# Gate/up weight lows by accumulating transfers, activations kept in DRAM, sums shared between two engines, in a hybrid decoder layer

## The chip, the cores and the metric

The kernel runs on one core of one Trainium2 chip. The metric is the device time of one execution in microseconds (us), and the number compared is the median over runs. A core has five engines that run their own instruction streams and wait for each other by semaphores: TensorE (PE in the profile; PEld is its weight load), VectorE (DVE), ScalarE (ACT), GpSimd (POOL) and SyncE (SP, which here only issues transfers). Transfers between DRAM and the on-chip memory are carried by 16 DMA engines.

## The reference

One decoder layer in float32 over 512 tokens of width 1024: a mixer (dilated attention and retention side by side), cross attention to a memory of 256 tokens, and a gated feed-forward block of hidden width 2816. Each block normalises its input, and normalises its output before it is added to the running `x`. The change lies mostly in the last block:

```
def swiglu(h, w_gate_up, w_down):
    g, u = jnp.split(h @ w_gate_up, 2, axis=-1)
    return (jax.nn.silu(g) * u) @ w_down
...
y = swiglu(rms_norm(x, pre_ffn_g[l]), w_gate_up[l], w_down[l])
x = x + rms_norm(y, post_ffn_g[l])
```

## The kernel before

**Precision.** TensorE multiplies operands of type fp32r, which keep fewer bits than float32. Each float32 operand is therefore held as a high part (`h` at the end of the tile's name: the value cast to fp32r) and a low part (`l`: the value minus its high part), and each product is three matmuls, high by high, high by low and low by high (`mm3`, L84 to L86). The helper `split` makes the two parts: ScalarE casts (L90), VectorE subtracts (L91).

**The feed-forward block.** The hidden width is cut into 22 pieces of 128. For each piece `f` one 1 MB block of weights holds four quarters `a11, a12, a22, a21` of 512 columns each. The first two pieces are computed plainly (`plain`, `plain_load`). The other 20 run in `step(f)`, which takes seven products of half the tokens instead of eight (a Strassen form). Some products use quarters of the weights as they are (`wa`), some use sums of quarters (`sums`, then split into `wb`: s1 = a21 + a22, s3 = a11 - a21, s2 = s1 - a11, s4 = a12 - s2); likewise for the activations (`B11`, `B21`, `B22`, `T1` to `T4`). Each product is 4 x 3 matmuls of 128x128 by 128x256. They accumulate in three PSUM banks, `p`, `q` and `r`, each holding two products side by side.

In `step(f)` TensorE runs products 1, 2, 4, 6, 5, 7, 3. The seventh product writes the first half of `p` again, so it must wait until ScalarE has copied that half (L879) and VectorE has read the other half of the same bank (L883). The third product writes the second half of `r`, behind VectorE's read of the first (L920). Between these, the same step prepares weights for later pieces: GpSimd makes the four sums of block `f + 2` (L116 to L119), ScalarE and VectorE split `wa` and `wb` of block `f + 1` (`blocks_split`, four calls), SP fetches block `f + 3` (L108). It also finishes the piece before: VectorE adds (L887), ScalarE applies Silu (L888), VectorE multiplies gate and up into the activation tile `af` (L894).

**What sets the order.** The steps run inside `tc.manual_schedule()` (L985): there each engine executes its instructions in the order in which the program writes them, so an instruction that waits holds up all that stands behind it on its engine. Everywhere else a planner orders the instructions by their place in the program and by what is ready. Tiles come from pools with a fixed number of buffers; a tile that takes a freed buffer waits for the last user of that buffer. `up` has 20 buffers of 8 KB a partition; `rawp` has two for each of its tags (`raw`, `sums`).

**Behind the steps** comes the down projection: 11 weight chunks (`w_dn`), each fetched, split and multiplied; activations are split by `split_a` (ScalarE casts L1002, GpSimd subtracts L1003). The last four chunks are done block of tokens by block of tokens, and behind each block `residual` (L645) takes squares on ScalarE, a reciprocal root on VectorE, and adds to `x`. Ahead of the feed-forward block, `mem_block` does the same for cross attention, and `to_b` transposes the normed tokens and makes the `B` and `T` operands.

Of the kernel before, what the change touches and what calls it, by code (L numbers as in the profile page):

```python
# [19 lines left out]
P = 128  # L20
# [18 lines left out]
def hybrid_layer(ctx, tc, t, out):  # L39
# [59 lines left out]
    loaded = {}  # L99
# [3 lines left out]
    blocks = {}  # L103

    def blocks_fetch(f):
        chunks.remove(("w_gu", f))
        raw = rawp.tile([P, 2048], F32, tag="raw", name=uname("raw"))
        nc.sync.dma_start(raw, t["w_gu"][f])  # L108
        blocks[f] = [raw]

    def blocks_sum(f):
        raw = blocks[f][0]
        a11, a12, a22, a21 = (raw[:, i * 512:(i + 1) * 512] for i in range(4))
        sums = rawp.tile([P, 2048], F32, tag="sums", name=uname("sums"))
        s2, s4, s1, s3 = (sums[:, i * 512:(i + 1) * 512] for i in range(4))
        nc.gpsimd.tensor_add(s1, a21, a22)  # L116
        nc.gpsimd.tensor_sub(s3, a11, a21)
        nc.gpsimd.tensor_sub(s2, s1, a11)
        nc.gpsimd.tensor_sub(s4, a12, s2)  # L119
        blocks[f] += [sums, pair("wa"), pair("wb")]  # L120

    def blocks_split(f, i):
        raw, sums, wa, wb = blocks[f]
        src, w, c0, n = ((raw, wa, 1024, 512), (raw, wa, 0, 1024), (sums, wb, 1024, 1024), (sums, wb, 0, 1024))[i]
        split(src[:, c0:c0 + n], *part(w, c0, n))

    def load(pieces=1, swap=False):
        key = chunks.pop(0)
        src = t[key[0]][key[1]]
        raw = rawp.tile([P, 2048], F32, tag="raw", name=uname("raw"))  # L130
        w = pair("w")
        n = 2048 // pieces
        for i in range(pieces):
            c = slice(i * n, (i + 1) * n)
            nc.sync.dma_start(raw[:, c], src[:, c])
# [509 lines left out]
    def residual(pss, b, g, e=None, cuts=((0, 512), (512, 512))):  # L645
# [4 lines left out]
        for i, (c0, n) in enumerate(cuts):  # L650
            c = slice(c0, c0 + n)
            ps = pss[c0 // 512][:, c0 % 512:c0 % 512 + n]
            nc.scalar.activation(junk()[:, :n], ps, AF.Square, accum_out=ss[:, i:i + 1])
            e.tensor_scalar(v, ss[:, i:i + 1], 1.0 / D, v if i else EPS, op0=ALU.mult, op1=ALU.add)
            nc.vector.tensor_mul(z[:, c], ps, g[:, c])
# [159 lines left out]
    def mem_block(b, mid=None):  # L815
        e = nc.vector
        residual(out_proj((b,), o_lhs, wo, nat, "o2", 0, mid)[b], b, g3, e)
        return normed(b, g4, e)

    def to_b(h, b):  # L820
# [15 lines left out]
        b12 = work("b12").rearrange("p (k s) -> p k s", k=4)  # L836
        split(pv[0], *bview("B12", c0))
        split(pv[1], *bview("B22", c0))
        nc.vector.tensor_sub(t1, pv[0], braw[:, 0, :, c0:c0 + P])
        nc.scalar.copy(b12, pv[0])  # L840
        nc.vector.tensor_sub(t2, pv[1], t1)
        nc.vector.tensor_sub(t3, pv[1], b12)
# [12 lines left out]
    af = []  # L855
# [14 lines left out]
    def ffn_p12(f):  # L870

        w, p = blocks[f][2:], bank("p")
# [16 lines left out]

    def ffn_mult(f):  # L890
        s1, c, u = ffn.pop(f)[2:5]
        if f % 4 == 0:
            af.append(unit("af"))
        nc.vector.tensor_mul(af[-1][:, (f % 4) * S:(f % 4 + 1) * S], c, u)  # L894

    def step(f):
        nxt = f + 1 < FT
        ffn_p12(f)
        w, p, s1, c, u = ffn[f]
        if f + 2 < FT:  # L900
            blocks_sum(f + 2)
        if f > PRE:
            ffn_done(f - 1)
        if nxt:
            blocks_split(f + 1, 0)
# [11 lines left out]
        product(6, w, r[:, :H])  # L917
        if nxt:
            blocks_split(f + 1, 2)
        nc.vector.tensor_add(s1[:, H:], s1[:, :H], r[:, :H])  # L920
        product(5, w, q[:, H:])
        if nxt:
            blocks_split(f + 1, 3)
# [6 lines left out]
        del blocks[f]  # L930
# [24 lines left out]
    for f in range(PRE):  # L955
        for j in range(2):
            plain(f, j, 0, pg[f][j])
        if f == 0:
            late_splits = [to_b(hb, 2)]
# [171 lines left out]
```

## Time and profile before

| | us |
|---|---|
| median of 3 runs | 834.13 (832.35 to 834.33) |
| the profiled execution, its own time | 835.61 |
| its span, first to last instruction | 833.8 |
| TensorE busy in the span | 797.6 |
| VectorE | 553.2 |
| ScalarE | 351.0 |
| GpSimd | 245.8 |

Rows of the profile read: line of the kernel, engine, operation, output tile `<-` input tiles, shapes, count, then busy time and mean time of one. In a row of the timeline the first number is the start in us from the span's start and the second the time it took; brackets give how long the engine was idle just before and what ended that. In a row of the waits: who waited `<-` for whom, total us, times, longest. In a row of windows: the stretch, then busy time and instruction count of each engine, the granted TensorE clock as a share of full speed, the mean busy share of the DMA engines, and GB/s. Consecutive matmuls overlap, so their pace is read from their starts, not from their durations.

### The profile page before, as it was taken

What the parts mean: (1) busy time and instruction counts of PE and PEld (TensorE: products, weight loads), DVE (VectorE), ACT (ScalarE), POOL (GpSimd) and SP (SyncE); (2) the same over time, 40 slices, a digit from 0 to 9 for tenths busy, and PEclk for the clock granted to TensorE, in tenths of its full rate; (3) what the DMA queues carried; (4) which work ended last, traced back from release to release, by engine and by line L of the source; (5) the groups of instructions that cost most, each with busy time, mean ns of one, the idle gap of its engine ahead of it and who ended that gap; (6) DMA issues with size and microseconds to landing.
All of it is one profiled execution on the core that took longest, in us unless ns stands there. A gap on an engine that the chain in (4) does not pass through costs nothing.

```text
span 833.8 us, 12068 instructions
## 1 busy us (share of the span) xinstructions
PE 797.6 (96%) x4828; PEld 698.0 (84%) x4828; DVE 553.2 (66%) x1012; ACT 351.0 (42%) x615; POOL 245.8 (29%) x190
## 2 busy tenths in 40 slices
PE   9979999999999999999999999989999899999996
PEld 7768888877777878999988989988889889888884
DVE  6595168764566657667568888889988886631244
ACT  6504333466464723446434734333344335524110
POOL 0261024410110100400029165555565542326000
PEclk9998999999999999999999999999999999999998
DMA  9516212221124440515004032222222224641011
GB/s 335 233 51 243 85 51 90 71 93 52 51 90 178 188 152 5 197 52 202 2 26 152 27 119 84 101 101 102 88 69 97 101 102 177 233 170 51 1 50 51
DMA packets 16648, 90.18 MB, mean 108 GB/s; under 512 B 2000, under 2 KB 2000, under 8 KB 8016
## 3 DMA queue, kind: packets, MB, share of 16 engines
q1 hardware_dynamic: 15872, 88.35, 28.9%
q10 hardware_dynamic: 720, 1.06, 0.3%
q8 instruction: 38, 0.62, 0.3%
q14 instruction: 18, 0.15, 0.1%
HBM read 85.21 MB, written 4.19 MB: 107 GB/s over the span
## 4 chain that ended last, share of the span: by engine, by line
PE 53%; DVE 29%; issue 8%; ACT 5%; POOL 3%; DMA 2%; DVEq 0%; SPq 0%; ACTq 0%; POOLq 0%
DVE wal L91 7%; PE dn L85 5%; PE dn L86 5%; PE dn L84 5%; DVE af L894 3%; DVE wl L91 3%; DVE wbl L91 3%; PE o L85 2%; PE o L86 2%; PE o L84 2%; PE oT L507 2%; DMA raw<-in_w_out 1%; PE q L85 1%; PE q L86 1%; PE q L84 1%
## 5 line engine op out<-in xcount | busy, mean ns | idle before, releaser
L91 DVE TENSOR_TENSOR wl<-raw,wh 128x1024 fp32r<-128x1024 f32 (+1 forms) x91 | 112.9, 1273 | 69.0 <-ACT wh L90 45.2
L90 ACT CAST wh<-raw 128x1024 fp32r<-128x1024 f32 (+1 forms) x91 | 90.3, 1039 | 73.0 <-DMA raw<-in_w_in 36.6
L91 DVE TENSOR_TENSOR wal<-raw,wah 128x512 fp32r<-128x512 f32 (+1 forms) x40 | 66.4, 1661 | 24.7 <-ACT wah L90 24.7
L85 PE MATMUL dn<-wl,ah 128*128 128x512 f32 x176 | 68.6, 390 | 0.3 <-DVE wl L91 0.3
L86 PE MATMUL dn<-wh,al 128*128 128x512 f32 x176 | 68.5, 389 | 0.0
L84 PE MATMUL dn<-wh,ah 128*128 128x512 f32 x176 | 67.7, 389 | 0.0
L888 ACT ACTIVATE c<-c 128x512 f32<-128x512 f32 x20 | 12.6, 632 | 124.6 <-DVE c L887 124.6
L91 DVE TENSOR_TENSOR wbl<-sums,wbh 128x1024 fp32r<-128x1024 f32 x40 | 57.0, 1425 | 0.0
L116 POOL TENSOR_TENSOR sums<-raw 128x512 f32<-128x512 f32 x20 | 25.9, 1294 | 91.6 <-DMA raw<-in_w_gu 66.6
L1003 POOL TENSOR_TENSOR al<-af,ah 128x512 fp32r<-128x512 f32 x22 | 32.8, 1519 | 54.6 <-ACT ah L1002 54.5
L84 PE MATMUL p<-bB,wah 128*128 128x256 f32 x160 | 45.3, 283 | 0.0
L85 PE MATMUL p<-bB,wah 128*128 128x256 f32 x160 | 45.3, 283 | 0.0
L86 PE MATMUL p<-bB,wal 128*128 128x256 f32 x160 | 45.3, 283 | 0.0
L90 ACT CAST wbh<-sums 128x1024 fp32r<-128x1024 f32 x40 | 39.9, 1049 | 0.0
L85 PEld LDWEIGHTS dn<-wl,ah 128*128 128x128 f32 x176 | 33.0, 188 | 7.7 <-DVE wl L91 0.7
L84 PEld LDWEIGHTS dn<-wh,ah 128*128 128x128 f32 x176 | 33.0, 188 | 6.8
L86 PEld LDWEIGHTS dn<-wh,al 128*128 128x128 f32 x176 | 33.0, 188 | 6.7
L84 PE MATMUL p<-bT,wbh 128*128 128x256 f32 x80 | 23.8, 298 | 14.3 <-DVE c L883 14.3
L119 POOL TENSOR_TENSOR sums<-raw,sums 128x512 f32<-128x512 f32 x20 | 36.2, 1810 | 1.6
L85 PE MATMUL q<-hhl,wh 128*128 128x256 f32 x128 | 36.2, 284 | 0.2 <-DVE hhl L91 0.2
L84 PE MATMUL q<-hhh,wh 128*128 128x256 f32 x128 | 35.8, 284 | 0.3 <-ACT hhh L90 0.3
L86 PE MATMUL q<-hhh,wl 128*128 128x256 f32 x128 | 36.1, 283 | 0.0
(330 smaller groups left out, 2569.8 us busy)
## 6 DMA issues: line engine op xcount, KB each, us to landing
raw<-in_w_gu SPq DMA_DIRECT2D x22, 1024.0 KB, 4.8
raw<-in_w_in SPq DMA_DIRECT2D x12, 1024.0 KB, 4.8
raw<-in_w_dn SPq DMA_DIRECT2D x11, 1024.0 KB, 4.7
raw<-in_w_kv SPq DMA_DIRECT2D x8, 1024.0 KB, 4.7
x<-in_x SPq DMA_DIRECT2D x4, 1024.0 KB, 8.8
raw<-in_w_out SPq DMA_DIRECT2D x4, 1024.0 KB, 5.6
raw<-in_w_q SPq DMA_DIRECT2D x4, 1024.0 KB, 4.8
raw<-in_w_o SPq DMA_DIRECT2D x4, 1024.0 KB, 4.8
```

Of the source, the lines that this page charges most:

```text
L84: nc.tensor.matmul(o, lhsT=sh, rhs=mh, start=start, stop=False)
L85: nc.tensor.matmul(o, lhsT=sh, rhs=ml, start=False, stop=False)
L86: nc.tensor.matmul(o, lhsT=sl, rhs=mh, start=False, stop=stop)
L90: nc.scalar.copy(hi, src)
L91: nc.vector.tensor_sub(lo, src, hi.bitcast(F32))
L116: nc.gpsimd.tensor_add(s1, a21, a22)
L119: nc.gpsimd.tensor_sub(s4, a12, s2)
L507: nc.tensor.matmul(oTb[pr][rows, kb * P:S], lhsT=av[:, kb * 512 + h * AD:kb * 512 + (h + 1) * AD], rhs=u[:, off[kb]:off[kb] + S - kb * P], ...
L888: nc.scalar.activation(c, c, AF.Silu)
L894: nc.vector.tensor_mul(af[-1][:, (f % 4) * S:(f % 4 + 1) * S], c, u)
L1003: nc.gpsimd.tensor_sub(lo[:, c], af[i][:, c], hi[:, c].bitcast(F32))
```

## The change

1. The low part of `wa` is no longer a subtraction on VectorE (or on GpSimd for the two plain pieces). ScalarE writes the high part and then its negative into the low tile, and a transfer issued by GpSimd adds the weights from DRAM onto it (`accum_op=ALU.add`). This is done for block `f + 2` in step `f`, so three pairs of `wa` are alive.
2. Of the four sums s1 and s2 move to VectorE; s3 and s4 stay on GpSimd. The `sums` tile comes from the pool `up`.
3. The product of gate and up is stored to a DRAM tile `ad` by SP and loaded back by `split_a` in the down stage.
4. The fetch of block `f + 3` is issued at the start of the step; in the last three steps it fetches the first chunks of `w_dn`, the first of which is split in the last step, and the first activations are split between the last two steps.
5. In `residual` the multiplication by the gain stands ahead of the operation that waits for the squares. `mem_block` runs its residual and norm at high priority. `to_b` of the third token block does its subtractions on GpSimd, with ScalarE copying out of PSUM.
6. The DRAM loads of `x` stand behind the loop over chunks, and the reserved DMA scratch goes back to its default size.

```
+    def blocks_sum(f, names):
+        if f not in sums:
+            sums[f] = unit("sums")
...
+            e = nc.gpsimd if name in ('s3', 's4') else nc.vector
...
+    def blocks_a(f, n=1536, m=768):
+        w = was[f] = pair("wa")
+        for c0 in range(0, n, m):
+            c = slice(c0, c0 + m)
+            nc.scalar.copy(w[0][:, c], raws[f][:, c])
+        for c0 in range(0, n, m):
+            c = slice(c0, c0 + m)
+            nc.scalar.mul(w[1][:, c], w[0][:, c].bitcast(F32), -1.0)
+        nc.gpsimd.dma_start(w[1][:, :n], t["w_gu"][f][:, :n], accum_op=ALU.add)
+
+    def blocks_b(f, i):
+        if f not in wbs:
+            wbs[f] = pair("wb")
+        split(sums[f][:, i * 1024:(i + 1) * 1024], *part(wbs[f], i * 1024, 1024))
...
+            nc.vector.tensor_mul(z[:, c], ps, g[:, c])
             e.tensor_scalar(v, ss[:, i:i + 1], 1.0 / D, v if i else EPS, op0=ALU.mult, op1=ALU.add)
-            nc.vector.tensor_mul(z[:, c], ps, g[:, c])
...
+        pss = out_proj((b,), o_lhs, wo, nat, "o2", 0, mid)[b]
+        with tc.high_priority(600):
+            residual(pss, b, g3, nc.vector)
+            return normed(b, g4, nc.vector)
...
+    def keep(f, v):
+        nc.sync.dma_start(ad[:, f * S:(f + 1) * S], v)
+
     def ffn_mult(f):
...
+        c, u = ffn.pop(f)[3:5]
+        nc.vector.tensor_mul(c, c, u)
+        keep(f, c)
 
     def step(f):
         nxt = f + 1 < FT
+        two = f + 2 < FT
         ffn_p12(f)
         w, p, s1, c, u = ffn[f]
-        if f + 2 < FT:
-            blocks_sum(f + 2)
+        if f + 3 < FT:
+            blocks_fetch(f + 3)
+        else:
+            fetch(("w_dn", f + 3 - FT))
         if f > PRE:
             ffn_done(f - 1)
-        if nxt:
-            blocks_split(f + 1, 0)
+        if two:
+            blocks_sum(f + 2, ("s3", "s1", "s2"))
         ffn_c1(f)
         if f > PRE:
             ffn_mult(f - 1)
         if nxt:
-            blocks_split(f + 1, 1)
-        if f + 3 < FT:
-            blocks_fetch(f + 3)
+            blocks_b(f + 1, 1)
+        else:
+            load()
         ffn_c11(f)
         q, r = bank("q2"), bank("r")
         ffn[f] += (r,)
         product(4, w, q[:, :H])
         product(6, w, r[:, :H])
+        if two:
+            blocks_sum(f + 2, ("s4",))
         if nxt:
-            blocks_split(f + 1, 2)
+            blocks_b(f + 1, 0)
+        if two:
+            blocks_a(f + 2)
         nc.vector.tensor_add(s1[:, H:], s1[:, :H], r[:, :H])
         product(5, w, q[:, H:])
-        if nxt:
-            blocks_split(f + 1, 3)
...
+    blocks_a(2)
+    blocks_sum(2, ("s3", "s1", "s2", "s4"))
+    blocks_fetch(3)
...
+        blocks_b(2, 1 - f)
...
+    blocks_a(3)
+    blocks_sum(3, ("s3", "s1", "s2", "s4"))
     blocks_fetch(4)
...
         for f in range(PRE, FT):
             step(f)
+            if f == FT - 2:
+                split_a(0)
...
-    nc = _bacc.Bacc("TRN2", target_bir_lowering=False, num_devices=1, dynamic_dma_scratch_size=1024)
+    nc = _bacc.Bacc("TRN2", target_bir_lowering=False, num_devices=1)
```

More of the change, by code (lines that the diff above doesn't have):

```diff
@@ L111, in blocks_sum @@
[L111 to L120, printed above, removed]
@@ L870, in ffn_p12 @@
     def ffn_p12(f):
-        w, p = blocks[f][2:], bank("p")
+        w, p = (was[f], wbs[f]), bank("p")
         product(1, w, p[:, :H])
@@ L909, in step @@
         if nxt:
-            blocks_split(f + 1, 1)
-        if f + 3 < FT:
-            blocks_fetch(f + 3)
+            blocks_b(f + 1, 1)
+        else:
+            load()
         ffn_c11(f)
@@ L929, in step @@
         product(3, w, r[:, H:])
-        del blocks[f]
+        for d in (raws, was, sums, wbs):
+            d.pop(f, None)
     PRE = 2
@@ L984, in hybrid_layer, with split_a @@
         nc.sync.dma_start(xd[b * P:(b + 1) * P, :], x[b])
+    aT = {}
+    def split_a(i):
+        hi, lo = pair("a")
+        n = min(4, FT - 4 * i)
+        v = unit("af")
+        nc.sync.dma_start(v[:, :n * S], ad[:, 4 * i * S:(4 * i + n) * S])
+        for j in range(n):
+            c = slice(j * S, (j + 1) * S)
+            nc.scalar.copy(hi[:, c], v[:, c])
+            nc.gpsimd.tensor_sub(lo[:, c], v[:, c], hi[:, c].bitcast(F32))
+        aT[i] = hi, lo
     with tc.manual_schedule():
```

120 lines of the change are left out of this document (53 added, 67 removed).

## The prediction

> **What bounds the kernel now.** I read the busy times first (TensorE, "PE", leads), then TensorE's waits, then the feed-forward stage in order of time. TensorE's own waits:
>
> ```profile
> PE p L84 <- DVE c L883: 14.3, 17, 1.6
> ...
> PE r L84 <- DVE s L920: 4.2, 9, 0.5
> ...
> PE tp L827 <- DVE h L664: 0.9, 1, 0.9
> ```
>
> Nearly all of TensorE's waiting for VectorE ("DVE") lies in one place: the seventh product of a feed-forward step (`p`, L84) waits for the addition L883. Four moments of TensorE's timeline size it: first matmul of the first step, first of a step in the middle, last before that step's stall and first behind it, and first of the down projection:
>
> ```profile
> 479.24 0.28 PE L84 MATMUL p<-bB,wah 128*128 128x256 f32 x1
> ...
> 570.68 0.28 PE L84 MATMUL p<-bB,wah 128*128 128x256 f32 x1
> ...
> 577.76 0.28 PE L86 MATMUL q<-bT,wbl 128*128 128x256 f32 x1
> 578.90 0.36 PE L84 MATMUL p<-bT,wbh 128*128 128x256 f32 x1 [0.87 <-DVE c L883]
> ...
> 705.41 0.63 PE L84 MATMUL dn<-wh,ah 128*128 128x512 f32 x2
> ```
>
> From 570.68 to 577.76 lie 59 intervals (products 1, 2, 4, 6, 5 are 5 x 12 = 60 matmuls): 0.12 us each. A step has 84 matmuls, so 10.08 us without a stall. The 20 steps take 705.41 - 479.24 = 226.17 us, 11.31 each; at 10.08 they would take 201.6. So 24.6 us are lost to stalls: that is what can be won here. Why L883 is late, from VectorE in the same step:
>
> ```profile
> 571.53 0.41 DVE L887 TENSOR_TENSOR c<-c,r 128x256 f32<-128x256 f32 x1
> 573.14 1.33 DVE L91 TENSOR_TENSOR wal<-raw,wah 128x512 fp32r<-128x512 f32 x1 [1.21 <-ACT wah L90]
> 574.40 1.79 DVE L894 TENSOR_TENSOR af<-c,u 128x512 f32<-128x512 f32 x1
> 576.11 2.31 DVE L91 TENSOR_TENSOR wal<-raw,wah 128x1024 fp32r<-128x1024 f32 x1
> 578.35 0.41 DVE L883 TENSOR_TENSOR c<-s,p 128x256 f32<-128x256 f32 x1
> 578.68 1.21 DVE L91 TENSOR_TENSOR wbl<-sums,wbh 128x1024 fp32r<-128x1024 f32 x1
> 579.82 0.41 DVE L920 TENSOR_TENSOR s<-s,r 128x256 f32<-128x256 f32 x1
> ```
>
> L883 runs 7.67 us into the step (578.35 - 570.68); the product wants it by 7.20 (60 x 0.12). Ahead of it stand two `wal` subtractions and the multiplication L894, stretched. What stretches them is GpSimd ("POOL"), making four sums at that time:
>
> ```profile
> 571.38 1.30 POOL L116 TENSOR_TENSOR sums<-raw 128x512 f32<-128x512 f32 x1 [3.71 <-DMA raw<-in_w_gu]
> 572.64 1.29 POOL L117 TENSOR_TENSOR sums<-raw 128x512 f32<-128x512 f32 x1
> 573.88 1.76 POOL L118 TENSOR_TENSOR sums<-sums,raw 128x512 f32<-128x512 f32 x1
> 575.72 1.62 POOL L119 TENSOR_TENSOR sums<-raw,sums 128x512 f32<-128x512 f32 x1
> ```
>
> The same two VectorE operations where GpSimd happened to be idle:
>
> ```profile
> 475.99 0.68 DVE L974 TENSOR_TENSOR af<-sg,u 128x512 f32<-128x512 f32 x1
> ...
> 483.67 1.23 DVE L91 TENSOR_TENSOR wal<-raw,wah 128x1024 fp32r<-128x1024 f32 x1 [1.80 <-ACT wah L90]
> ```
>
> 0.68 against 1.79, 1.23 against 2.31: 1.1 us for each VectorE operation with two SBUF operands that meets GpSimd's. The second row is of the first step, which did not stall.
>
> **The step after the change.** Times from the step's first matmul; ScalarE ("ACT") of the same step:
>
> ```profile
> 571.97 0.63 ACT L888 ACTIVATE c<-c 128x512 f32<-128x512 f32 x1 [6.49 <-DVE c L887]
> 572.51 0.60 ACT L90 CAST wah<-raw 128x512 fp32r<-128x512 f32 x1
> 573.76 0.37 ACT L879 COPY s<-p 128x256 f32<-128x256 f32 x1 [0.65 <-PE p L86]
> 574.03 1.05 ACT L90 CAST wah<-raw 128x1024 fp32r<-128x1024 f32 x1
> 574.97 2.00 ACT L90 CAST wbh<-sums 128x1024 fp32r<-128x1024 f32 x2
> ```
>
> VectorE loses the two `wal` subtractions (0.68 + 1.23 unstretched) and gains s1 and s2 (2 x 0.68). Ahead of the L883 addition stand: L887 (0.3 to 0.7; bound by product 3 of the step before), s1, s2, the multiplication (3 x 0.68: 2.7, if Silu, 0.75 to 1.4, is done, and it is), and one `wbl` (1.2). That one waits for its cast, which waits behind the copy L879; the copy waits for product 2 (573.76 - 570.68 = 3.08, unchanged), so the cast ends at 4.4 and `wbl` at 5.6. L883 then ends at 6.0, against the 7.20 wanted: 1.2 us to spare. GpSimd keeps two sums. s3 can stretch s1 or s2, s4 the multiplication, each by 1.1: the multiplication then ends at 4.9, `wbl` at 6.1 and L883 at 6.5, still in time. The second `wbl` follows L883 and ends near 7.2 to 7.7, L920 at 8.1 at most; product 3 (`r`) wants it at 8.64. So TensorE sets the step: 10.08 us, and the 24.6 us go.
>
> The Trainium skill, SBUF — State Buffer, "Who interferes with whom", says that a VectorE instruction with two SBUF inputs contends with a GpSimd instruction that reads SBUF, and that the later one blocks fully. It speaks against putting s1 and s2 on VectorE beside s3. The stretched rows agree, at 1.1 us each; by a full block of 1.30 a time, L883 would end at 6.9, still ahead of 7.20.
>
> ScalarE per step: the 1536-wide cast becomes two of 768 and two multiplications by -1 of 768. Between 0.60 for 512 and 1.05 for 1024, 768 is 0.83, so 3.3 in place of 1.65, behind the two `wbh` casts (which end at 5.4): done at 8.7. With Silu, copy and `wbh` ScalarE holds 6.3 of 10.08 us, and nothing that TensorE wants is behind this batch before the next step.
>
> GpSimd: s3, s4 (3.5 at most, by 2 x 1.76) and the issue of the accumulating transfer, which waits for the multiplications until 8.7. Queued behind it is only s3 of the next block, and s4's cast comes a step later. Issuing has no row: above nothing, and at most as long as GpSimd's longest row here (1.76). I take 1 us.
>
> SP: the fetch moves ahead in the step, onto a buffer freed in the step before, so it does not hold the 256 KB store of activations behind it; that store waits for the multiplication and holds up only the next fetch, a step away. In the last three steps these fetches bring down-projection weights. The third waits until the first has been split, in the last step; behind it the last stores wait, read only at the end of the down stage. The split in the last step (two casts, two subtractions) takes the place of the `wb` work that the last step lacks. Activations come back by six loads hidden behind the down stage, where a pair of weight chunks occupies TensorE for some 22 us (705.41 to the last residual at 826.68, by 11 chunks). The x loads now follow that stage's loop, with four chunks to come.
>
> **The accumulating transfer** is the price that no row shows. A block is issued at 8.7 + 1 = 9.7 of its step and needed 20.4 after that step's start (third matmul, two steps on): 10.7 us are there. The nearest rows, for the stage and for the plain 1 MB loads:
>
> ```profile
> 492.00:680.00 188.00, 170.71 (x1376) 166.10 (x1376) 167.23 (x179) 73.26 (x101) 108.06 (x69) 1.00 0.26 90
> DMA to landing us min/median/max: 4.1/4.8/10.1
> ```
>
> 0.26 x 188 us for 90 GB/s x 188 us = 16.9 MB is 2.9 us of the 16 engines per MB: 3.0 for a 1.05 MB fetch (the other 1.8 of the 4.8 is fixed), 0.8 for the store, and 2.3k for the 0.79 MB accumulated, where k says how many times a plain byte an accumulated one costs. k = 1 if the addition is free; k = 3 if the source read, the read of the destination and the write each cost a transfer. I take the middle, 2: two reads and one write. Then the engines are busy 3.0 + 0.8 + 4.6 = 8.4 of 10.08 us, and the transfer lands in 1.8 + 4.6 = 6.4, or 9.4 behind a fetch: in time. At k = 1 it lands in 4.1 to 7.1. At k = 3 the engines need 10.7 a step and TensorE loses about 0.6 x 20 = 12 us of the 24.6.
>
> The Trainium skill, Collectives: The Full Stack, "The bandwidth ceiling: the fold count and why AG ≠ RS ≠ AR", says that a reducing transfer runs at half a copy's rate because it reads two sources, not because the addition costs. No row of before shows one; by the page k is 2 and the sum stays as it is.
>
> **Around the steps.** Before them GpSimd's eight `wal` subtractions go:
>
> ```profile
> 433.54 11.94 POOL L948 TENSOR_TENSOR wal<-raw,wah 128x512 fp32r<-128x512 f32 x8 [80.60 <-ACT wah L947]
> 433.89 3.20 DVE L659 SCALAR_TENSOR_TENSOR x<-z,pry,x 128x512 f32<-128x512 f32 x2
> ```
>
> They stretch the residual L659, on whose chain the 0.9 us wait of `tp` hangs. I book -1.0. Against it: ScalarE gets eight 512 multiplications and the batches of blocks 2 and 3, about 10 us, into a stage half empty of ScalarE work; the high priority keeps the residual ahead. The first accumulated block of the steps proper, block 3, is cast among the last things there (near 482), so it lands at 490 to 492 and is wanted at 489.6: +1. Moving one block's additions to GpSimd (six operations, 8 to 10 us) stays behind the next block's products; between -0.5 and +3, taken as 0.
>
> At the end the product z moves ahead of the wait for the squares:
>
> ```profile
> 826.68 0.21 DVE L654 TENSOR_SCALAR pv<-ps,pv 128x1 f32<-128x1 f32 x1 [4.69 <-ACT junk L653]
> 826.82 0.68 DVE L655 TENSOR_TENSOR z<-dn,g 128x512 f32<-128x512 f32 x1
> 827.41 0.14 DVE L163 TENSOR_SCALAR pry<-pv 128x1 int32<-128x1 int32 x1
> ```
>
> L163 need no longer wait for it: -0.6 (827.41 - 826.82), nothing hidden.
>
> Sum: -24.6 - 1.0 - 0.6 + 1, and +1.7 for small stalls that I can't place (0.08 a step): -23.5. The profiled execution's own time, 835.61, becomes 812.1; it is 1.48 above the median of the runs, 834.13, which becomes 810.6. With nothing lost it is 834.1 - 26.2 = 807.9.
>
> **Rivals.** (a) The accumulating transfer is half late (k near 3): TensorE's wait moves from L883 to the first product's low weights, `wal`; 10.5 to 11.0 us a step, 818 to 828. For it: the engines would be over 80% busy. (b) VectorE's order still holds L883 up, since `wbl` now stands ahead of it and hangs on ScalarE; with all of s3 and s4 falling on s1 to `wbl`, 3 x 1.1, L883 ends at 7.6, 0.4 late, 20 x 0.4 lost: 819. Against it: s3 has run by the time s1 starts. (c) Slower: accumulation by the engines is so dear that it sets the step. 3.8 + 2.3k passes 11.31 at k = 3.3; at k = 4 a step takes 13.0, and 834.1 + 20 x 1.7 - 1.6 (the gains at both ends) gives 866. Nothing in the profile excludes it. (d) The transfers and all else fit, but the stage before the steps loses as much as is won, over 20 us of new ScalarE lateness: no difference, 834. Little speaks for it: ScalarE has room.
>
> **Chances.** Forecast 0.63, (a) 0.12, (b) 0.07, (c) 0.15, (d) 0.03. About 0.3% (2.5 us) can't be told from no change. Faster 0.81, same 0.04, slower 0.15. Range 807 to 828: forecast, (b) and most of (a).
>
> **What will show it.** Right: step starts 10.1 us apart, no wait of `p` for the addition that L883 makes now, a 1024 `wbl` near 1.2 us, accumulations landing in 6 to 10 us. Wrong: TensorE waiting for a transfer into `wal` at a step's start (a, c), L883 ending later than 7.2 into the step (b), or the first step starting well behind 479 (d).

## The result and the profile after

The changed kernel takes 814.43 us (median of four runs, 813.49 to 814.72); the kernel before, measured beside it, 833.64 (832.35 to 834.33). The ratio is 0.977 with a 95% interval of 0.975 to 0.979. The forecast of 810.6 had the direction, and the time of the steady steps as well as what sets it; it was 3.8 us too low.

The profiled execution of the changed kernel has a span of 811.7 us against 833.8, so 22.1 us less; the medians differ by 19.2. The profiled execution of before (835.61) took longer than any of its four runs here and that of after was the shortest of its runs, so the total is taken from the medians, and the profiles are read for where it lies.

TensorE's largest wait from the feed-forward block on in the profile after (total, times, longest, in us):

```profile
PE p L84 <- DVE c L910: 3.8, 2, 2.1
```

L910 is the addition that was L883. TensorE waited for it 17 times before; now twice, in the first step and in the last (1.67 us there). First matmul of the first step, of its seventh product, of the second step, of one in the middle, of the last, and of the down projection:

```profile
476.51 0.28 PE L84 MATMUL p<-bB,wah 128*128 128x256 f32 x1
486.39 0.35 PE L84 MATMUL p<-bT,wbh 128*128 128x256 f32 x1 [2.15 <-DVE c L910]
490.06 0.28 PE L84 MATMUL p<-bB,wah 128*128 128x256 f32 x1
560.62 0.28 PE L84 MATMUL p<-bB,wah 128*128 128x256 f32 x1
671.50 0.28 PE L84 MATMUL p<-bB,wah 128*128 128x256 f32 x1
683.46 0.40 PE L84 MATMUL dn<-wh,ah 128*128 128x512 f32 x1
```

From 490.06 to 671.50 lie 18 steps of 10.08 us: not one has a stall. The first step takes 13.55 us and the last 11.96, where both took 10.08 before. The 20 steps together take 206.95 us in place of 226.17.

VectorE in the step that begins at 560.62, and the sum s4 on GpSimd beside it:

```profile
561.15 0.98 DVE L123 TENSOR_TENSOR sums<-raw 128x512 f32<-128x512 f32 x1
562.17 0.69 DVE L125 TENSOR_TENSOR sums<-sums,raw 128x512 f32<-128x512 f32 x1
562.78 0.68 DVE L922 TENSOR_TENSOR c<-c,u 128x512 f32<-128x512 f32 x1
565.05 1.23 DVE L91 TENSOR_TENSOR wbl<-sums,wbh 128x1024 fp32r<-128x1024 f32 x1 [1.58 <-ACT wbh L90]
566.19 0.41 DVE L910 TENSOR_TENSOR c<-s,p 128x256 f32<-128x256 f32 x1
```
```profile
562.94 1.68 POOL L125 TENSOR_TENSOR sums<-raw,sums 128x512 f32<-128x512 f32 x1 [1.36 <-DVE sums L125]
```

The addition ends 5.98 us into the step (566.60 - 560.62), where the forecast had 6.0 and the product wants it by 7.20. The multiplication (L922) takes 0.68 instead of 1.79, although s4 still runs beside it: it begins 0.16 us before s4, and here s4 is the longer one (1.68 us, where GpSimd's sums of this size took 1.30 and 1.29 in two rows before).

The transfers, by queue (packets, MB, share of 16 engines) and by issue (KB each, median us to landing), and their issue on GpSimd (times; total us, mean ns):

```profile
q1 hardware_dynamic: 19904, 99.89, 33.3%
q0 software_dynamic: 3168, 17.83, 12.0%
...
L135 POOL DMA_DIRECT2D wal<-in_w_gu x22 | 19.6, 889 | 176.3 <-ACT wal L134 117.7
...
wal<-in_w_gu POOLq DMA_DIRECT2D x20, 768.0 KB, 7.5
```

An accumulated MB costs 0.120 x 811.7 / 17.83 = 5.46 us of the 16 engines, one of the plain queue q1 0.333 x 811.7 / 99.89 = 2.71: 2.0 times as much.

### The profile page after: what moved, and what is told of

Its sections match the earlier page's. It is cut to its first block, busy times and chain, and to the rows that moved or that the text cites. A ratio compares the mean times of both kernels' runs of the same rounds, so it can differ in the third digit from the quotient of the medians.

```text
span 811.7 us, 12194 instructions
## 1 busy us (share of the span) xinstructions
PE 790.5 (97%) x4828; PEld 696.5 (86%) x4828; DVE 503.5 (62%) x1007; ACT 384.4 (47%) x664; POOL 196.8 (24%) x169
## 3 DMA queue, kind: packets, MB, share of 16 engines
q1 hardware_dynamic: 19904, 99.89, 33.3%
q0 software_dynamic: 3168, 17.83, 12.0%
## 4 chain that ended last, share of the span: by engine, by line
PE 76%; DVE 12%; issue 4%; POOL 3%; ACT 3%; DMA 1%; DVEq 0%; SPq 0%; ACTq 0%; POOLq 0%
PE dn L84 5%; PE dn L86 5%; PE dn L85 5%; PE p L84 3%; PE o L85 3%; PE p L86 3%; PE p L85 3%; PE o L84 3%; PE o L86 3%; PE q L85 3%; PE q L86 3%; PE q L84 3%; DVE wl L91 3%; PE r L84 2%; PE r L85 2%
## 5 line engine op out<-in xcount | busy, mean ns | idle before, releaser
L91 DVE TENSOR_TENSOR wl<-raw,wh 128x1024 fp32r<-128x1024 f32 (+1 forms) x91 | 118.0, 1330 | 66.1 <-ACT wh L90 39.6
L91 DVE TENSOR_TENSOR wbl<-sums,wbh 128x1024 fp32r<-128x1024 f32 x40 | 51.2, 1280 | 30.3 <-ACT wbh L90 30.3
L135 POOL DMA_DIRECT2D wal<-in_w_gu x22 | 19.6, 889 | 176.3 <-ACT wal L134 117.7
L1022 POOL TENSOR_TENSOR al<-af,ah 128x512 fp32r<-128x512 f32 x22 | 36.1, 1672 | 43.9 <-ACT ah L1021 43.9
L125 POOL TENSOR_TENSOR sums<-raw,sums 128x512 f32<-128x512 f32 x20 | 34.1, 1704 | 25.4 <-DVE sums L125 25.4
L134 ACT ACTIVATE wal<-wah 128x768 fp32r<-128x768 f32 (+1 forms) x48 | 36.6, 810 | 0.0
L131 ACT CAST wah<-raw 128x768 fp32r<-128x768 f32 (+1 forms) x48 | 35.9, 804 | 0.0
```

The source lines that it names most:

```text
L91: nc.vector.tensor_sub(lo, src, hi.bitcast(F32))
L125: e.tensor_sub(*{"s2": (s2, s1, a11), "s3": (s3, a11, a21), "s4": (s4, a12, s2)}[name])
L131: nc.scalar.copy(w[0][:, c], raws[f][:, c])
L134: nc.scalar.mul(w[1][:, c], w[0][:, c].bitcast(F32), -1.0)
L135: nc.gpsimd.dma_start(w[1][:, :n], t["w_gu"][f][:, :n], accum_op=ALU.add)
L1022: nc.gpsimd.tensor_sub(lo[:, c], v[:, c], hi[:, c].bitcast(F32))
```

## The experiments

Two questions were open: which part of the change frees the steady steps (the order, the lead of two blocks, the transfers, the moved sums), and where the 3.8 us against the forecast went. Unless a row is quoted, times are medians and ratios are against the kernel before beside it. "First step" and "last step" are from first matmul to first matmul, as above.

### All four sums on GpSimd again

```
-            e = nc.gpsimd if name in ('s3', 's4') else nc.vector
+            e = nc.gpsimd
```

> The changed kernel (814.4 us, 10.08 us a step) with all four sums back on GpSimd; the lows stay with the accumulating transfers. Theory: what mattered is that less stands ahead of the addition that product 7 waits for. VectorE loses s1 and s2 (2 x 0.7) but meets four GpSimd sums again, so the multiplication and the first wbl are stretched by 1.1 each; the wbl waits for its cast until 4.4, ends near 6.7, the addition at 7.1, against 7.20 wanted: 10.1 to 10.3 us a step, 814 to 819 us. Rival, that the two sums on VectorE carry the gain (contention with GpSimd is the cause): the steps go back to 10.6 or more, 825 us or more.

Measured: 817.13 us, ratio 0.980 (0.978 to 0.982). The steady steps take 10.08 us, so the sums' move does not free them. What it is worth lies at the ends: the first two steps take 15.29 and 11.19 us, the last 12.50. In the last TensorE waits 2.20 us for the addition. In the first two it waits for the transfer, 3.1 us in all; GpSimd issues it among the sums, and it lands later (10.0 us in the median against 7.5):

```profile
wal<-in_w_gu POOLq DMA_DIRECT2D x20, 768.0 KB, 10.0
```

### Lows by VectorE, two blocks ahead, no accumulating transfer

The multiplications by -1 and the transfer go; VectorE subtracts the lows of block `f + 2` behind the addition that follows product 5, out of the way of L910 (which is L914 in this kernel).

```
         product(5, w, q[:, H:])
         nc.vector.tensor_add(c[:, H:], s1[:, H:], q[:, H:])
+        if two:
+            blocks_low(f + 2)      # VectorE: wal = raw - wah, two of 768
```

> The changed kernel with the lows of block f + 2 subtracted by VectorE (two of 768 columns a step, behind the addition of product 5) instead of multiplied by -1 on ScalarE and accumulated by a transfer. Theory A, that the order is what mattered (lows no longer ahead of the addition, a block more of lead) and VectorE has room: its work in a step goes from 7.6 to 9.5 us, below 10.08, so the steps stay at 10.1 to 10.3 and the time within 0.5% of 814. Theory B, that VectorE had to be relieved of the lows and the transfers carry the gain: the subtractions push the late additions and the next step's work back, steps of 10.6 or more, 825 us or more.

Measured: 828.16 us, ratio 0.992 (0.990 to 0.995). The steady steps fall from about 11.4 to between 10.38 and 10.56, nearly as far as with the transfers; but the first step takes 18.33 us and begins at 481.32. With both its two sums and the lows VectorE has little room left. What is late is no longer the addition (it ends 6.55 us into the step that begins at 551.79) but VectorE's read of `r` (L960 in this kernel), on which product 3 waits (TensorE's weight load, 500 to 680 us):

```profile
PEld r L84 <- DVE s L960: 4.5, 16, 0.4
```

The window 510 to 600 us of this kernel, and of the kernel after (columns: window, its length, then busy time and count of PE, PEld, DVE, ACT, POOL, granted clock, DMA share, GB/s):

```profile
510.00:600.00 90.00, 89.40 (x730) 87.78 (x730) 84.67 (x115) 39.14 (x54) 30.41 (x18) 1.00 0.36 132
```
```profile
510.00:600.00 90.00, 90.00 (x753) 90.00 (x752) 62.84 (x99) 52.60 (x72) 34.03 (x27) 1.00 0.80 208
```

VectorE is busy 84.67 of 90 us against 62.84; the transfers take the difference off VectorE, for a DMA share of 0.80 in place of 0.36.

### Order and lead alone

Both edits above together: all sums on GpSimd, as before the change, and the lows on VectorE, as before the change. What stays of the change in the steps is the order of VectorE's work, the lead of two blocks, and the buffers and the earlier fetch that go with it.

```
+            e = nc.gpsimd                       # all four sums
...
+        if two:
+            blocks_low(f + 2)                   # VectorE, behind product 5's addition
```

> The changed kernel with both moves of work undone: all four sums on GpSimd and the lows of wa subtracted by VectorE, as before the change; what stays is the order (the lows of block f + 2, two of 768 columns, behind the addition of product 5; one wbl ahead of the addition that product 7 waits for) and the lead of two blocks. Theory: order and lead carry most of the gain in the steady steps. VectorE's own work is 7.6 + 1.9 - 1.4 = 8.1 us, stretched by four GpSimd sums to some 9.5: 10.1 to 10.5 us a step. Rival: it is the load on VectorE and its meeting with GpSimd; then the steps go back to 11 us and the time to 835 or more. Before the steps the lows of the first blocks crowd VectorE as when it alone took them (first step 4.8 us later and 4.8 us longer than in the changed kernel), so some 825 us in all by the theory.

Measured: 826.64 us, ratio 0.991 (0.988 to 0.994). The steady steps take 10.08 us (one, the ninth, 10.18); from the first matmul of the second step to that of the ninth, 7 x 10.08, and VectorE in the ninth:

```profile
499.61 0.28 PE L84 MATMUL p<-bB,wah 128*128 128x256 f32 x1
...
570.17 0.28 PE L84 MATMUL p<-bB,wah 128*128 128x256 f32 x1
```
```profile
573.22 1.00 DVE L926 TENSOR_TENSOR c<-c,u 128x512 f32<-128x512 f32 x1 [0.70 <-ACT c L919]
574.60 1.23 DVE L91 TENSOR_TENSOR wbl<-sums,wbh 128x1024 fp32r<-128x1024 f32 x1 [0.37 <-ACT wbh L90]
575.74 0.41 DVE L914 TENSOR_TENSOR c<-s,p 128x256 f32<-128x256 f32 x1
576.07 2.35 DVE L91 TENSOR_TENSOR wbl<-sums,wbh 128x1024 fp32r<-128x1024 f32 x1
```

The addition ends 5.98 us into the step, as with the transfers, although VectorE still makes every low and GpSimd still makes all the sums. So it is the order that frees the steady steps: the lows stand behind the addition instead of in front of it, and a lead of two blocks allows that. Neither the accumulating transfers nor the move of two sums is needed there. GpSimd's sums also fall elsewhere: in the step shown none runs from 573.67 to 576.04, so the multiplication and the `wbl` ahead of the addition take 1.00 and 1.23 us, and the `wbl` behind it is the stretched one (2.35). That by itself does not decide it: with all sums on GpSimd and the lows by transfer, the two take 1.21 and 1.72 us in the step that begins at 563.52, and the addition still ends 6.48 us into it. No run takes the order apart from the earlier fetch.

What the two are needed for is the head of the loop, the transfers above all (828.16 us without them alone, 817.13 without the moved sums alone). The first step begins at 478.73 here and takes 20.88 us, 2.2 later and 7.3 longer than in the kernel after. Ahead of that step's addition VectorE has the lows of blocks 2 and 3 as well, four of 768 elements, 3.71 and 3.98 us for the pairs. The second step begins 9.55 us later than after (499.61 against 490.06); the spans, 821.4 and 811.7 us, differ by 9.7, so in the profiles the head of the loop is nearly all that the transfers and the moved sums are worth. The profiled execution, 823.17 us, is the shortest of this kernel's four runs; the medians differ by 12.2, and where the other 2.5 lie isn't shown.

### Lows by GpSimd, two blocks ahead, no transfer

```
-            nc.gpsimd.dma_start(w[1][:, :n], t["w_gu"][f][:, :n], accum_op=ALU.add)
+            nc.gpsimd.tensor_sub(w[1][:, c], raws[f][:, c], w[0][:, c].bitcast(F32))
```

> The changed kernel with the lows of block f + 2 subtracted by GpSimd (two of 768 columns a step, two blocks ahead) instead of accumulated by a transfer; no multiplication by -1. If any way off VectorE will do: GpSimd has 3.3 us of sums and gets two subtractions of some 1.9 each, 7.1 of 10.08 us, VectorE's second wbl is stretched by 1.1, nothing that TensorE waits for: steps of 10.08 us, 814 to 820 us with the first steps. If the meeting of VectorE and GpSimd is what costs: steps above 10.4, 822 us or more.

Measured: 823.44 us, ratio 0.988 (0.986 to 0.990). The steady steps take 10.08 us but for the second and the fourth (11.40 and 11.00); the first takes 19.43. The steps have room for the lows on this engine too; the head of the loop has not.

### The same transfers without the addition

Only the transfer's type differs; it leaves out the addition, so the low parts are the raw weights.

```
-        nc.gpsimd.dma_start(w[1][:, :n], t["w_gu"][f][:, :n], accum_op=ALU.add)
+        nc.gpsimd.dma_start(w[1][:, :n], t["w_gu"][f][:, :n])
```

> The changed kernel with the accumulating transfer replaced by a plain one of the same bytes from GpSimd: it leaves out the addition, so the low parts and the output are not the reference's, and only the time is read. Forecast of the price: an accumulated byte costs twice a plain one (k = 2). The transfers of GpSimd's queue then take half the engines' time (12.0% of the span becomes 6%), and land in 4 to 6 us instead of 7.5. The steps stay at 10.08, since the landing was hidden. Rival: most of the 7.5 us is the way from GpSimd (issue, software descriptors), then landing stays above 6.5.

Measured: one execution, 813.36 us, with the same steps. The price of the addition by itself:

```profile
q0 software_dynamic: 3168, 17.83, 6.2%
...
L135 POOL DMA_DIRECT2D wal<-in_w_gu x22 | 12.8, 580 | 182.1 <-ACT wal L134 118.6
...
wal<-in_w_gu POOLq DMA_DIRECT2D x20, 768.0 KB, 5.0
```

0.062 x 811.6 / 17.83 = 2.82 us of the engines per MB against 5.46: a factor of 1.94 by queue shares, landing 5.0 against 7.5 us, issue 0.58 against 0.89 us. None of it is on TensorE's path in the steady steps.

### Lows one block ahead

```
-        if two:
-            blocks_a(f + 2)
+        if nxt:
+            blocks_a(f + 1)
...
-    blocks_a(3)
```

> The changed kernel with the lows accumulated one block ahead instead of two (the batch for block f + 1 in step f). Theory: the transfer is hidden only by the second step. It is issued 8.8 us into the step, lands 7.5 later, and the third matmul of the next step wants it: a step of 16.0 to 16.5 us, some 930 us in all, with TensorE waiting for the transfer at the start of each step. Rival, that the transfer lands early enough for one block or that only the order counts: 10.1 to 11 us a step.

Measured: one execution, 984.87 us; steps of 17.3 to 20.5 us behind the first. TensorE waits for the transfer in each (6.9 us in the mean), so the lead of two is what hides it. The steps are some 2 us longer than that wait explains:

```profile
PE p L86 <- DMA wal<-in_w_gu: 132.0, 19, 9.5
```
```profile
594.41 0.55 PE L86 MATMUL p<-bB,wal 128*128 128x256 f32 x1 [6.64 <-DMA wal<-in_w_gu]
594.76 0.42 PE L84 MATMUL p<-bB,wah 128*128 128x256 f32 x1
...
597.10 0.38 PE L86 MATMUL p<-bB,wal 128*128 128x256 f32 x1
597.32 0.29 PE L84 MATMUL p<-bB,wah 128*128 128x256 f32 x1
...
598.40 0.28 PE L84 MATMUL q<-bT,wah 128*128 128x256 f32 x1
```

Behind a wait of 6.64 us the matmuls come 0.21 us apart (11 intervals from 594.76 to 597.10), and 0.12 apart from 597.32 on (9 intervals to 598.40). The granted clock from 500 to 600 us is 0.79 in the mean, where it is 1.00 in the kernel after from 510 to 600. The Trainium skill, TensorE: Matmul & The Clock Gate, "HAM oscillation — how this bites in real kernels", says that TensorE runs at half its clock for a while behind an idle gap of more than about 3.4 us. These rows agree in kind: little more than half the pace for 2.9 us behind this wait, and for 2.9 to 6.1 us behind the other waits for the transfer in this run. The runs do not show that length as the threshold: in the first step of this same run the slow pace follows a wait of 2.15 us, and in the kernel after, behind a wait of the same length, it does not (0.12 us from the second interval on).

### The last step: activations loaded and cast earlier

In the kernel after, the first activations are loaded back and split between the last two steps, where ScalarE's casts wait for the load and VectorE's split of the first `w_dn` chunk meets GpSimd's subtractions:

```profile
675.93 4.12 DVE L91 TENSOR_TENSOR wl<-raw,wh 128x1024 fp32r<-128x1024 f32 x2 [0.36 <-ACT wh L90]
679.97 0.41 DVE L910 TENSOR_TENSOR c<-s,p 128x256 f32<-128x256 f32 x1
```
```profile
672.47 11.21 POOL L1022 TENSOR_TENSOR al<-af,ah 128x512 fp32r<-128x512 f32 x7 [11.43 <-ACT ah L1021]
```

The addition ends 8.9 us into the step, 1.7 behind its time. The edit loads the activations two steps earlier and splits them inside the step before the last, in the place that `blocks_a` leaves empty:

```
             step(f)
-            if f == FT - 2:
-                split_a(0)
+            if f == FT - 4:
+                load_a(0)
...
         if two:
             blocks_a(f + 2)
+        if f == FT - 2:
+            split_a(0)
```

> The changed kernel with the first activations loaded two steps earlier, and cast and subtracted in the last step but one, where GpSimd has no sums. Theory: the last step took 11.96 instead of 10.08 us since the two wl subtractions ahead of the addition (4.12 us for two) meet GpSimd's subtractions of the activations. Then the last step falls to 10.1 to 10.4 and the time by 1.5 to 1.9 us. Rival: two wl subtractions ahead of the addition are too much on their own, the last step stays above 11.

Measured: 812.11 us (811.80 to 813.48), ratio 0.974 (0.972 to 0.976), the fastest of all kernels here. The last step takes 10.20 us (671.56 to 681.76):

```profile
675.99 2.36 DVE L91 TENSOR_TENSOR wl<-raw,wh 128x1024 fp32r<-128x1024 f32 x2 [1.93 <-ACT wh L90]
678.26 0.41 DVE L910 TENSOR_TENSOR c<-s,p 128x256 f32<-128x256 f32 x1
```

The same two subtractions take 2.36 us in place of 4.12. That is the 1.8 us of the last step.

### The first step: its sums and lows earlier

```
     blocks_fetch(2)
+    blocks_a(2)
+    blocks_sum(2, ("s3", "s1", "s2", "s4"))
+    blocks_fetch(3)
...
     late_splits.append(to_b(hc, 3))
-    blocks_a(2)
-    blocks_sum(2, ("s3", "s1", "s2", "s4"))
-    blocks_fetch(3)
+    blocks_sum(3, ("s3", "s1", "s2", "s4"))
```

> The changed kernel with the sums and lows of block 2 and the fetch of block 3 written ahead of the plain products, and the sums of block 3 ahead of their second half. Theory: the first step took 13.55 us because block 3's sums are still being made in it (two s1 and two s2 on VectorE, two s4 on GpSimd), which holds up its wbl and the addition. Made earlier, the first step falls to 10.1 to 11 and the time by 2.5 to 3.5 us. Rival: there is no room in the stage before (buffers or VectorE are full), the work only moves and the first step starts later by as much.

Measured: 813.81 us, ratio 0.977 (0.974 to 0.980): as the kernel after. The planner ran 5 of the 24 matmuls of the step's first two products among the plain ones, the second step begins at 488.34 instead of 490.06, and the third at 500.03 instead of 500.13. In between lies a new wait of 1.3 us for the transfer. It is for the low part of block 3, the first one accumulated for the steps proper. In the kernel after TensorE does not wait for it; with the second step 1.7 us earlier it does. The head of the loop has two limits close to one another. The profiled execution is the longest of the four (817.52 us), and where it is longer than the kernel after is the last step: 16.02 us in place of 11.96. The casts of the activations, which wait for their load, start at 673.37 instead of 671.71, and TensorE waits longer for the addition, with matmuls 0.21 us apart up to the end of the step:

```profile
682.15 0.56 PE L84 MATMUL p<-bT,wbh 128*128 128x256 f32 x1 [3.40 <-DVE c L910]
```

### The first step: the third block's operands on VectorE, or the third lows on GpSimd

Two edits on the load of VectorE there. One takes `to_b` of the third block back to VectorE, the other (on top of the edit of the last step) gives three of the eight `T` lows to GpSimd.

```
-            late_splits = [to_b(hb, 2, nc.gpsimd)]
+            late_splits = [to_b(hb, 2)]
```

> The changed kernel with the operands of the third token block made on VectorE again. If GpSimd's part in them is what leaves VectorE room before the steps: VectorE gets five operations of 0.7 there, and the first step starts or ends 2 to 4 us later, 816 to 819 us. Rival: GpSimd's queue, held by them until 467 us, is what makes the sums of blocks 2 and 3 late; then the first step gets shorter than 13.55 and the time falls by 1 to 3 us.

Measured: 813.91 us, ratio 0.976 (0.974 to 0.978); the first step takes 13.49 us, the next begins at 490.21. No difference.

```
-        return lambda: [split(v, *bview(n, c0)) for v, n in ((t2, "T2"), (t1, "T1"), (t4, "T4"), (t3, "T3"))]
...
+                (nc.gpsimd if n == "T3" or (n == "T1" and e is nc.gpsimd) else nc.vector).tensor_sub(lo, v, hi.bitcast(F32))
```

> The changed kernel with the first activations loaded, cast and subtracted earlier (as in the run of that edit, whose last step took 10.20 us) and with three of the eight low parts of the T operands subtracted by GpSimd in place of VectorE, where GpSimd waits for a transfer before the steps. Theory: the first step is late because VectorE is full from 464 to 489 us; three subtractions of 0.7 to 0.9 less take 2 us off it, so the first step falls to 11 to 12.5 us and the time to some 810. Rival: the sums of block 4 wait for their transfer, or GpSimd's own queue for the subtractions, and the first step stays at 13 or more: 812.

Measured: 813.76 us, ratio 0.976 (0.974 to 0.978), not better than the edit of the last step alone (812.11); the first step takes 15.58 us instead of 13.55. The lows on VectorE in the kernel after, and in this one:

```profile
470.21 7.11 DVE L91 TENSOR_TENSOR bT<-t,bT 128x512 fp32r<-128x512 f32 x8
```
```profile
470.22 7.50 DVE L875 TENSOR_TENSOR bT<-t,bT 128x512 fp32r<-128x512 f32 x5
```

Eight take 7.11 us (0.89 each); the five that are left take 7.50 (1.50 each) since GpSimd runs the other three beside them. VectorE gains nothing from giving them away.

### The multiplication in `residual` behind the wait, and no priority

```
-            nc.vector.tensor_mul(z[:, c], ps, g[:, c])
             e.tensor_scalar(v, ss[:, i:i + 1], 1.0 / D, v if i else EPS, op0=ALU.mult, op1=ALU.add)
+            nc.vector.tensor_mul(z[:, c], ps, g[:, c])
```

> The changed kernel with the multiplication by the gain back behind the operation that waits for the squares, in all residuals. As predicted for the edit: the tail from TensorE's last matmul to the span's end would be 0.6 us longer than the changed kernel's 8.4. As the trace of the changed kernel reads, where the multiplication itself waits for ScalarE's square of the same bank: no longer, rather 0.1 shorter.

Measured: one execution, 814.78 us. From the last matmul to the end it takes 8.25 us, 8.37 in the kernel after, 7.93 in the kernel before: the edit of `residual` gains nothing.

```
-        with tc.high_priority(600):
+        if True:
```

> The changed kernel without the high priority in mem_block. If the priority is what keeps the residuals ahead of ScalarE's new weight work, the first step starts 1 us or more later than 476.5 us and TensorE waits for a normed block; if GpSimd's absence from that stage did it, the first step starts within 0.5 us of 476.5 and the time stays within 0.3% of 814.

Measured: 815.31 us, ratio 0.979 (0.976 to 0.981). The first step begins at 476.74 instead of 476.51 and takes 14.24 instead of 13.55. The whole difference of the first step lies behind its wait for the addition, which is as long as in the kernel after (2.15 us): here the matmuls come 0.21 us apart for 3.1 us behind it, there 0.12. So the priority is worth 0.9 us at most by the medians, which this comparison can't tell from nothing; the earlier start comes without it.

## Why the prediction was right, point by point

**What bounded the kernel.** Right. With the stalls in front of product 7 gone, 18 steps take 10.08 us, the 84 x 0.12 of the forecast; over 20 steps that would be the whole 24.6 us.

**Why L883 was late.** Right in the instructions it named, half right in what followed. The two `wal` subtractions ahead of it and the stretched multiplication made it late; but they did not have to leave VectorE. With the order alone they stay on VectorE and the addition is as early (5.98 us). The forecast of the step rests on "VectorE loses the two `wal` subtractions", and it never priced the order by itself.

**The step after.** L910 at 5.98 against 6.0; both rows of `wbl` at 1.22 and 1.23; GpSimd stretched s1 by 0.3 and not by the 1.1 allowed for. Rival (b), VectorE's order, did not come about in the kernel after. In the kernel with two sums and the lows on VectorE a late VectorE does cost 0.3 a step, but at product 3 and not at the addition that (b) names.

**The accumulating transfer.** The value taken, k = 2, measured 2.0 against the plain loads of SP's queue and 1.94 against the same transfer without the addition. By the Trainium skill, Collectives: The Full Stack, "The bandwidth ceiling: the fold count and why AG ≠ RS ≠ AR", it would be 2; the trace agrees. Landing took 7.5 us (6.4 to 9.4 forecast), the issue 0.89 (1 forecast). The engines are busy for 0.80 of the time from 510 to 600 us, where the forecast's 8.4 of 10.08 is 0.83. So rivals (a) and (c), which need k near 3 or above, are refuted. That the landing stays hidden hangs on the lead of two blocks: one block ahead the same transfer gave steps of 17 to 20 us.

**The prelude.** Booked at -1.0; the first step begins 2.73 us earlier (479.24 to 476.51). Of that 1.3 lies ahead of every stage that the change's edits run in: the same small matmul `bc` begins at 106.4 us before and 105.1 after, and why isn't shown. The rest, 1.4, is near the size booked: TensorE's wait of 0.9 for `tp` is gone, and the pair of residual operations that GpSimd stretched takes 1.41 us in place of 3.20:

```profile
432.37 1.41 DVE L676 SCALAR_TENSOR_TENSOR x<-z,pry,x 128x512 f32<-128x512 f32 x2
```

Rival (d), a prelude that loses it all, is refuted for the changed kernel; without the transfers it comes half true: the first step loses 10.8 us. The third block's additions on GpSimd, taken as 0, came to nothing either way.

**The first step: the term that was mis-sized.** Booked at +1, for block 3's transfer landing late at the start of the second step. It cost 3.47 (13.55 against 10.08), inside the first step, by VectorE. From 464.5 to 489 us, after and (below) before:

```profile
464.50:489.00 24.50, 21.60 (x172) 20.85 (x173) 24.21 (x29) 20.71 (x31) 15.10 (x11) 1.00 0.64 170
```
```profile
464.50:489.00 24.50, 24.26 (x201) 23.83 (x200) 21.30 (x27) 15.47 (x23) 7.36 (x5) 1.00 0.25 86
```

VectorE is busy for 24.21 of 24.50 us where it had 3.2 to spare, and GpSimd for 15.10 where it had 7.36. In the kernel after, the sums of blocks 3 and 4 stand right ahead of the addition:

```profile
481.22 1.28 DVE L123 TENSOR_TENSOR sums<-raw 128x512 f32<-128x512 f32 x2
482.42 1.28 DVE L125 TENSOR_TENSOR sums<-sums,raw 128x512 f32<-128x512 f32 x2
...
485.84 0.41 DVE L910 TENSOR_TENSOR c<-s,p 128x256 f32<-128x256 f32 x1
```

The addition ends 9.7 us into the step, 2.5 behind its time. Part of that is the earlier start. Counted from the span's start the addition is only 1.0 us later than before (486.25 against 485.22, the row below), while the step begins 2.73 earlier; and the second step begins at 490.06, where it began at 489.32. So what was won ahead of the loop was lost again as a wait in its first step: the two terms, booked at -1 and +1, came to -2.73 and +3.47.

```profile
484.81 0.41 DVE L883 TENSOR_TENSOR c<-s,p 128x256 f32<-128x256 f32 x1
```

The lead of two blocks is not the cause: with the lows one block ahead TensorE waits just as long for the addition in the first step (14.32 us):

```profile
487.94 0.42 PE L84 MATMUL p<-bT,wbh 128*128 128x256 f32 x1 [2.15 <-DVE c L910]
```

Nor is it the move of the sums to VectorE by itself. With all sums on GpSimd the addition ends even later, 10.2 us into the step (486.79 - 476.57), since GpSimd's sums then stretch VectorE's lows of the `T` operands; TensorE does not wait for it there, because the transfer (2.25 us) and a `wbl` (0.51) have held it up before. The lows in that kernel, and in the kernel before, where GpSimd is idle from 471.9 on:

```profile
469.43 10.82 DVE L91 TENSOR_TENSOR bT<-t,bT 128x512 fp32r<-128x512 f32 x8 [1.44 <-ACT bT L90]
```
```profile
470.95 5.11 DVE L91 TENSOR_TENSOR bT<-t,bT 128x512 fp32r<-128x512 f32 x7
```

1.35 us each against 0.73. So VectorE pays for the sums in this stage, by making them or by GpSimd's running beside it; how the 2.5 us divide among the sums, the stretching and the earlier start stays open. The forecast costed the sums in a steady step, where there is room, and not here. The lateness of block 3 that it did book is real: it shows as a wait of 1.3 us when the second step begins earlier, and only then. A head of the loop with neither was not found: none of the three edits tried there gained by a measurable amount.

**The last step.** The split there was said to "take the place of the `wb` work" and booked at nothing; it cost 1.88. It is not the same work: GpSimd, which has no sums then, runs the activations' subtractions beside it. Putting them a step earlier gave 1.76 of it back in the trace; the median fell by 2.3 (814.43 to 812.11).

**The tail.** Booked at -0.6; it came to +0.44, and to +0.32 with the edit undone. About 0.3 of both lies behind the issue of the last store, 3.3 us from the span's end in both, 3.0 before. The multiplication was to run while VectorE waits for the squares. It waits for them itself:

```profile
803.43 0.60 ACT L670 ACTIVATE junk<-dn 128x512 bf16<-128x512 f32 x1 [4.75 <-PE dn L86]
...
803.92 0.19 ACT L670 ACTIVATION_READ_ACCUMULATOR junk<-dn 128x1 f32 x1
```
```profile
804.15 0.69 DVE L671 TENSOR_TENSOR z<-dn,g 128x512 f32<-128x512 f32 x1 [4.69 <-ACT junk L670]
```

It starts at 804.15, right behind ScalarE's operation on the same PSUM bank `dn`, which ends at 804.11, although it uses nothing of its result. The Trainium skill, PSUM — Partial Sum Buffer, "PSUM bank collisions raise a hardware error", says that no two engines may access one bank in the same partitions at once, two reads included, and that such accesses have to be put in order; the row agrees, though no run here puts the two reads on different banks. With that rule the step would have been booked at nothing.

**The sum.** By the profiled executions: -24.6 for the stalls, +3.5 and +1.9 for the first and the last step, -2.7 for the start of the first step, -0.6 in the down projection (not traced to a cause), +0.4 in the tail: -22.1, against -23.5 forecast. The +1.7 for small stalls was not needed in the steady steps. That the profiles came within 1.4 us is in part luck: the first and the last step and the tail were booked too low by 2.5, 1.9 and 1.0, and the small stalls, the start of the first step and the down projection too high by 1.7, 1.7 and 0.6. The other 2.4 of the 3.8 us come from the step from an execution to the median: the one profiled before stands 1.5 above its median, the one after 0.9 below.

## What to carry to other kernels

Before work is taken off a busy engine, try it behind the one instruction on which the bounding engine waits: here the order, with buffers for one block more of lead, freed every steady step by itself, and moving the work off paid only at the head of the loop. Cost a moved operation in each stage that runs it, first and last iteration too, by the room that the engines have there and not in the mean: 18 steps ran without a stall, the first lost 3.5 us and the last 1.9. A gain ahead of a loop counts only if the engine that feeds its first iteration comes earlier too: here the loop began 2.73 us earlier and its second step 0.74 later. Handing VectorE's operations to GpSimd beside it can give nothing back: three of eight moved, and the other five took as long as the eight.

## What the runs showed that was not expected

- A transfer that accumulates costs about twice a plain one of the same size in engine time (5.46 against 2.82 us per MB) and 1.5 times in landing (7.5 against 5.0 us for 768 KB) and in issue (0.89 against 0.58 us on GpSimd).
- Waits of about 7 us in each step cost more than their length: matmuls 0.21 instead of 0.12 us apart for 2.9 to 6.1 us behind one, and a mean granted clock of 0.79. Behind the first step's wait of 2.15 us the slow pace came in two runs (lows one block ahead; no priority) and not in others, so one such step can differ by 0.7 us with the same wait.
- A VectorE that is nearly full can be harmless, by its order. In the kernel with order and lead alone, from 510 to 600 us, it is busy for 79.90 of 90 us, TensorE for all 90:

```profile
510.00:600.00 90.00, 90.00 (x751) 89.96 (x751) 79.90 (x99) 38.55 (x54) 65.15 (x37) 1.00 0.37 132
```

  In the kernel before, from 500 to 600 us, VectorE is busy for 88.58 of 100 us, the same share, and TensorE for 91.73:

```profile
500.00:600.00 100.00, 91.73 (x741) 89.53 (x742) 88.58 (x98) 39.19 (x54) 56.84 (x36) 1.00 0.26 93
```
